# Two key buffers in the long-range attention, larger row and raw-weight rings in the last stage, first MLP chunk block by block

## The chip, the cores and the metric

The kernel runs on one core of one Trainium2 chip. The metric is the device time of one execution in microseconds (us); lower is better. A core has five engines that matter here: PE (TensorE, the matrix multiplier), DVE (VectorE), ACT (ScalarE), POOL (GpSimd) and SP (SyncE). Each runs its own list of instructions in order and waits on semaphores for the others. In this kernel SP issues every DMA, so it is one in-order queue for all loads and stores.

## The reference

One layer of a streaming encoder over a prompt of 2048 rows and a sample of 32 rows, width 1024, in float32:

```
z = rmsnorm(x) @ w_in                  # 3072 columns: q, k, v of group A and of group B
oa = diff_attn(qa, ka, va)             # 4 heads, two maps of 64 dims, values 128 wide, T5 bias,
                                       # weights = softmax(map 1) - lam * softmax(map 2), causal in chunks of 64
ob = band_attn(qb, kb, vb)             # 8 heads of 64, each chunk sees itself and 8 chunks before
h = x + concat(rmsnorm(oa)*(1-lam_init), rmsnorm(ob)) @ w_out
h = h + square(relu(rmsnorm(h) @ w_up)) @ w_down          # 1024 -> 4096 -> 1024
y = rmsnorm(h + sigmoid(h @ w_ple_gate) * (p @ w_ple_proj))
```

The sample attends to 128 cached keys and its own 32; y and the new keys and values are outputs.

## The kernel before

**Precision.** Every large matrix product is done with both operands split into a high part and a low remainder, and three matmuls per 128-deep slice (`mm3`, L186: hi·hi, hi·lo, lo·hi). A weight is therefore loaded raw (`wunit`, L177: tile "wr", two buffers), copied by ACT into the high part "wh" and subtracted by POOL, in pieces of 256 columns, into the low part "wl" (three buffers each). Activations are split in the same way: "cH"/"cL" for the MLP's input, "hH"/"hL" for the gate, "uh"/"ul" for the MLP's inner rows.

**Blocks.** The 2080 rows are four blocks (512, 512, 512, 544), taken as two halves, blocks 0 and 1, then 2 and 3. PE's product of one column block of 128 with one row block is 24 matmuls.

**Order.** The program text gives priorities; a scheduler with a timeline model writes the order of each engine's instructions once, when the program is built. On the chip each engine follows that order. So a change of a buffer count can move instructions of every engine, and SP's queue with them.

**Stages, in order of time.** Input norm and projections; short attention passes; band attention; then the long-range differential attention (`attn_a`, L511, with JA1 = [(4, 5), (6, 7, 8)] in pool a1), woven with the output projection, MLP and gate of the first half (about 1240 to 2080 us); then the last stage, from L1226: output projection of blocks 2 and 3 (`outproj`, L841), the gate of block 0 (`gate`, L988), the norms of blocks 2 and 3 (`cnorm`, L870), the MLP of both in 16 chunks (`mlp_up`, L917, `mlp_down`, L941), gate and final norm (`final`, L1039).

**Long-range attention.** `attn_a` runs each list of JA1 over the four heads g. A number j is a pair of query tiles of 128 rows (8 is the sample). For each head it loads the bias (ba), the keys (ka, hi and lo part on the two halves of the partitions; one buffer of 2 x 2208 columns; two or three DMAs per part) and then runs the pairs: queries (q, two buffers, four DMAs a pair), scores "s" (L567), maximum on DVE, exp on ACT, the difference of the two maps on DVE (L604), transposes, values (v), output "o". With (6, 7, 8) all 2208 keys are loaded, the last 160 (cache and sample) serving the sample alone. Eight passes, so seven changes from one head to the next.

**Rows of the last stage.** Tiles of one 128 x 544 row block, "tmp", form one ring of four. It is shared by the attention outputs that are to be split (`raw_o`, L802), the residual rows and squares of the output projection ("hd", L849, added on DVE at L860), the rows that the norm reads back (L879) and the MLP's relu results (L935).

**First MLP chunk.** `mlp_up` takes two columns f of 128 and both blocks of the half; the order is f, then block. So PE's order in the last stage is f0 of block 2, f0 of block 3, f1 of block 2, f1 of block 3. In the first half `mlp` is called with one block at a time.

Of the kernel before, what the change touches and what calls it, by code (L numbers as in the profile page):

```python
# [12 lines left out]
F32 = mybir.dt.float32  # L13
F32R = mybir.dt.float32r
# [5 lines left out]
P = 128  # L20
D = 1024
SP = 2048
SS = 32
# [110 lines left out]
class Kern:  # L134
    def __init__(self, tc, a):
        self.tc = tc
        self.nc = tc.nc
        self.a = a

    def dma(self, dst, src):  # L140
        if dst.dtype == F32R:
# [34 lines left out]

    def wunit(self, src, shape, hi_eng="act", lo_eng="pool"):  # L177
        nc = self.nc
        raw = self.wp.tile([P] + shape, F32, tag="wr", bufs=2, name="wr")
        self.dma(raw, src)  # L180
        hi = self.wp.tile([P] + shape, F32R, tag="wh", bufs=3, name="wh")
        lo = self.wp.tile([P] + shape, F32R, tag="wl", bufs=3, name="wl")
        self.split(hi, lo, raw, hi_eng, lo_eng)
        return hi, lo
# [326 lines left out]
    def attn_a(self, js, pool, ps_s, ps_t, ps_o):  # L511
        nc = self.nc
        last = 8 in js
        nk = KC if last else 256 * (js[-1] + 1)
        for g in range(4):
            ba = self.bias_a(pool, g)
            kt = pool.tile([P, 2, 1024 if self.small else KC], F32R, tag="ka", bufs=1, name="ka")
            for hl in range(2):
                src = self.kS[g, hl].rearrange("(m r) c -> r m c", m=2)
                for c0 in range(0, nk, 1024):  # L520
                    c1 = min(c0 + 1024, nk)
                    self.dma(kt[64 * hl : 64 * hl + 64, :, c0:c1], src[:, :, c0:c1])
            for j in js:
                self.attn_a_pair(g, j if j < 8 else None, kt, ba, pool, ps_s, ps_t, ps_o)

    def attn_a_pair(self, g, j, kt, ba, pool, ps_s, ps_t, ps_o):
        nc = self.nc
# [9 lines left out]
        for qi, t in enumerate(tiles):  # L537
# [25 lines left out]
            for bi, (k0, n, near) in enumerate(blocks):  # L563
                for m in range(2):
                    s = ps_s.tile([P, 512], F32, tag="s", name="s")[:nr, :n]
                    for hl in range(2):
                        nc.tensor.matmul(  # L567
                            s, q[:, m, hl, P * qi : P * qi + nr], kt[:, m, k0 : k0 + n], start=hl == 0, stop=hl == 1
                        )
                    dst = e[m][:nr, k0 - kb : k0 - kb + n]  # L570
                    nmx = nm[:nr, m, bi : bi + 1]
                    if near is None:
                        nc.vector.tensor_reduce(nmx, s, axis=AX.X, op=ALU.max, negate=True)  # L573
                        src = s
                    else:
                        nc.vector.tensor_tensor_reduce(
                            dst, s, ba[:nr, near : near + n], 1.0, -3e38, ALU.add, ALU.max, nmx
                        )
                        nc.vector.tensor_scalar(nmx, nmx, -1.0, None, op0=ALU.mult)
                        src = dst  # L580
                    nc.scalar.activation(dst, src, AF.Exp, bias=nmx, accum_out=z[:nr, m, bi : bi + 1])  # L581
# [218 lines left out]
                self.dma(self.pS[:, 1, k, t0 : t0 + n], lo[:, :n])  # L800

    def raw_o(self, wk, k, t0, n):  # L802
        t = wk.tile([P, BLK], F32, tag="tmp", bufs=4, name="oraw")[:, :n]
        self.dma(t, self.oT[:, k, t0 : t0 + n])
        return t

# [34 lines left out]
    def outproj(self, b, wk, oact, ps, acc):  # L841
        nc, a = self.nc, self.a
        n, t0 = BN[b], 512 * b
        W = a["w_out"][0]
        sq = wk.tile([P, BLK], F32, tag="acc", bufs=2, name="sqacc2")[:, :n]
        acc.append(sq)
        for d in range(8):
            wh, wl = self.wunit(W[:, P * d : P * d + P].rearrange("(k p) c -> p k c", p=P), [8, P])
            h = wk.tile([P, BLK], F32, tag="tmp", bufs=4, name="hd")[:, :n]  # L849
            self.dma(h, self.xT[:, d, t0 : t0 + n])  # L850
            for s0, sn in SUBS[b]:
                p = ps.tile([P, 512], F32, tag="mm", name="ops")[:, :sn]
                self.mm3(
                    p,
                    [
                        (wh[:, k], wl[:, k], oact[0][k][:, s0 : s0 + sn], oact[1][k][:, s0 : s0 + sn])
                        for k in range(8)
                    ],
                )
                nc.vector.tensor_tensor(h[:, s0 : s0 + sn], h[:, s0 : s0 + sn], p, op=ALU.add)  # L860
            if d == 0:
                nc.scalar.activation(sq, h, AF.Square)
            else:
                tmp = wk.tile([P, BLK], F32, tag="tmp", bufs=4, name="tmp")[:, :n]
                nc.scalar.activation(tmp, h, AF.Square)
                self.pool_tt(sq, sq, tmp, ALU.add)
            self.dma(self.hS[:, d, t0 : t0 + n], h)
            yield

    def cnorm(self, b, wk, act, out):  # L870
# [5 lines left out]
        r = wk.tile([P, BLK], F32, tag="r", bufs=2, name="rl")[:, :n]  # L876
        self.dma(r, self.rS[:, t0 : t0 + n])
        for k in range(8):
            tmp = wk.tile([P, BLK], F32, tag="tmp", bufs=4, name="tmp")[:, :n]  # L879
            self.dma(tmp, self.hS[:, k, t0 : t0 + n])  # L880
            nc.vector.scalar_tensor_tensor(
                tmp, tmp, self.g_mlp[:, k : k + 1], r, op0=ALU.mult, op1=ALU.mult
# [34 lines left out]
    def mlp_up(self, ch, nf, blocks, st, wk, up, mm):  # L917
        nc = self.nc
        Wu = self.a["w_up"][0]
        us = {}  # L920
        for f in range(nf):
            ft = nf * ch + f
            wh, wl = self.wunit(Wu[:, P * ft : P * ft + P].rearrange("(k p) c -> p k c", p=P), [8, P])
            for b in blocks:
                h, cH, cL = st[b]
                uh = up.tile([P, up.aw], F32R, tag="u", name="uh")
                ul = up.tile([P, up.aw], F32R, tag="u", name="ul")
                us[f, b] = (uh, ul)
                for s0, sn in SUBS[b]:
                    ps = mm.tile([P, 512], F32, tag="mm", name="ups")[:, :sn]  # L930
                    self.mm3(
                        ps,
                        [(wh[:, k], wl[:, k], cH[:, k, s0 : s0 + sn], cL[:, k, s0 : s0 + sn]) for k in range(8)],
                    )
                    r = wk.tile([P, BLK], F32, tag="tmp", bufs=4, name="relu")[:, :sn]  # L935
                    nc.scalar.activation(r, ps, AF.Relu)  # L936
                    nc.scalar.activation(r, r, AF.Square)
                    self.split(uh[:, s0 : s0 + sn], ul[:, s0 : s0 + sn], r, "act", "pool")
        return us

    def mlp_down(self, ch, nf, blocks, us, st, wk, mm):  # L941
# [154 lines left out]
    def run(self):  # L1096
        tc, nc, a = self.tc, self.nc, self.a
        with ExitStack() as top:
# [8 lines left out]
            cp = opened(top, "cp", 1)  # L1107
            self.dp = opened(top, "dp", 1, bass.MemoryType.DRAM)
            self.wp = opened(top, "wp", 3)
            mm = opened(top, "mm", MM, PSUM)  # L1110
            tp = mm
            psx = ExitStack()
# [112 lines left out]
            psx.close()  # L1225
            wk = opened(top, "wk4", 1)  # L1226
            fk = opened(top, "fk4", 1)
            self.gfin(fk)
            md = opened(top, "md", 8 - MM, PSUM, "right")
            act = Sized(opened(top, "acth", 4), BLK, True)  # L1230
# [75 lines left out]
```

## Time and profile before

| what | us |
| --- | --- |
| median of 3 runs | 3257.93 (3256.7 to 3264.15) |
| the profiled execution | 3256.49 |
| its span, first to last instruction | 3254.6 |
| PE busy in it | 3076.7 |
| DVE, ACT, POOL busy | 1557.3, 1693.7, 1706.8 |
| mean granted PE clock, as a share of full | 0.984 |

The time of a run is taken from outside; the span is what the profiler saw of one execution. A view of waits lists, for an engine, what its instructions waited for (tile, line, then the engine that let them go and what it wrote): total us, number of times, longest. A view of groups lists instructions of one line: count, busy time and mean ns, then idle time of the engine just before them with the releaser. A timeline gives start, length and instruction, with idle time before it in brackets. In a view of stretches each row is a piece of the span with the busy time of each engine, the granted PE clock (1.00 is full), the share of the DMA engines that was busy, and GB/s.

### The profile page before, as it was taken

The numbers are of one execution on the slowest core, as the hardware profiler recorded it, in microseconds if no ns is written. First come the engines' busy times: TensorE is split into PE (matmuls) and PEld (weight loads), VectorE is DVE, ScalarE is ACT, GpSimd is POOL, SyncE is SP. The second block draws the span as 40 slices with busy tenths as digits, with TensorE's granted clock in tenths as the row PEclk, the third lists the DMA queues.
The fourth block names the chain that finished last, engine by engine and source line by source line (L and its number), as shares of the span: only waits on it lengthen the run. The fifth ranks groups of instructions, "written<-read, shape, count | busy, mean of one in ns | idle before, by whom it ended". The sixth has DMA issues, their size and how long they took to land. (4 is left out here: it accounts for less than half of the span.)

```text
span 3254.6 us, 51557 instructions
## 1 busy us (share of the span) xinstructions
PE 3076.7 (95%) x17881; PEld 2692.7 (83%) x17881; DVE 1557.3 (48%) x3952; ACT 1693.7 (52%) x3717; POOL 1706.8 (52%) x2515
## 2 busy tenths in 40 slices
PE   6998999899999999999999999989899999999998
PEld 6877789789987887878788788868789999999988
DVE  5116786544465554676664565625442232223235
ACT  4226666776666765676665566544443222322245
POOL 5446766233245544565655455676854333433387
PEclk9999999999999999999999999999999999999999
DMA  7488786786788654554644544347531111111133
GB/s 232 165 259 246 226 244 206 213 259 202 215 239 229 187 146 118 152 156 138 199 122 135 137 123 136 121 143 233 150 113 46 46 46 46 46 46 46 47 94 103
DMA packets 519085, 489.02 MB, mean 150 GB/s; under 512 B 37885, under 2 KB 414017, under 8 KB 518825
## 3 DMA queue, kind: packets, MB, share of 16 engines
q1 hardware_dynamic: 518824, 485.73, 50.9%
q8 instruction: 142, 2.33, 0.3%
q14 instruction: 119, 0.97, 0.1%
HBM read 379.06 MB, written 110.49 MB: 150 GB/s over the span
## 5 line engine op out<-in xcount | busy, mean ns | idle before, releaser
L164 POOL TENSOR_TENSOR wl<-wr,wh 128x256 fp32r<-128x256 f32 x936 | 695.2, 774 | 489.4 <-ACT wh L169 453.1
L169 ACT ACTIVATE wh<-wr 128x1024 fp32r<-128x1024 f32 x338 | 357.2, 1057 | 598.5 <-PE dps L191 298.9
L971 DVE TENSOR_TENSOR h<-h,dps 128x512 f32<-128x512 f32 (+1 forms) x640 | 373.0, 585 | 575.0 <-PE dps L192 562.7
L154 POOL TENSOR_TENSOR wl<-wr,wh 128x256 fp32r<-128x256 f32 x416 | 301.8, 757 | 401.2 <-ACT wh L169 386.9
L190 PE MATMUL dps<-uh,wh 128*128 128x512 f32 (+1 forms) x1280 | 458.2, 358 | 7.1 <-DVE h L971 5.8
L190 PE MATMUL ups<-cH,wh 128*128 128x512 f32 (+1 forms) x1280 | 452.7, 354 | 5.7 <-ACT relu L936 4.5
L191 PE MATMUL ups<-cL,wh 128*128 128x512 f32 (+1 forms) x1280 | 451.5, 353 | 1.5 <-POOL cL L154 1.2
L192 PE MATMUL ups<-cH,wl 128*128 128x512 f32 (+1 forms) x1280 | 450.8, 352 | 0.0
L192 PE MATMUL dps<-uh,wl 128*128 128x512 f32 (+1 forms) x1280 | 450.1, 352 | 0.0
L191 PE MATMUL dps<-ul,wh 128*128 128x512 f32 (+1 forms) x1280 | 449.3, 351 | 0.0
L154 POOL TENSOR_TENSOR ul<-relu,uh 128x136 fp32r<-128x136 f32 (+1 forms) x320 | 198.9, 643 | 171.0 <-ACT uh L169 166.7
L190 PEld LDWEIGHTS dps<-uh,wh 128*128 128x128 f32 x1280 | 241.6, 189 | 39.7 <-DVE h L971 10.2
L190 PEld LDWEIGHTS ups<-cH,wh 128*128 128x128 f32 x1280 | 241.1, 188 | 38.6 <-ACT relu L936 4.7
L191 PEld LDWEIGHTS ups<-cL,wh 128*128 128x128 f32 x1280 | 241.6, 189 | 33.0 <-POOL cL L154 2.0
L192 PEld LDWEIGHTS dps<-uh,wl 128*128 128x128 f32 x1280 | 240.9, 188 | 33.6
L192 PEld LDWEIGHTS ups<-cH,wl 128*128 128x128 f32 x1280 | 241.3, 189 | 30.0
L191 PEld LDWEIGHTS dps<-ul,wh 128*128 128x128 f32 x1280 | 241.9, 189 | 26.5
L190 PE MATMUL qps<-aH,wh 128*128 128x512 f32 (+1 forms) x640 | 229.7, 359 | 11.0 <-ACT kr L432 3.4
L192 PE MATMUL qps<-aH,wl 128*128 128x512 f32 (+1 forms) x640 | 228.0, 356 | 0.0
L191 PE MATMUL qps<-aL,wh 128*128 128x512 f32 (+1 forms) x640 | 227.9, 356 | 0.0
L567 PE MATMUL s<-ka,q 128*128 128x256 f32 (+4 forms) x784 | 191.7, 346 | 30.8 <-DMA ka<-kS 10.1
L581 ACT ACTIVATE e<-s,nm 128x512 f32<-128x512 f32 (+3 forms) x256 | 154.9, 611 | 80.3 <-DVE nm L573 69.4
(218 smaller groups left out, 7075.0 us busy)
## 6 DMA issues: line engine op xcount, KB each, us to landing
wr<-w_up SPq DMA_DIRECT2D x96, 512.0 KB, 4.2
wr<-w_down SPq DMA_DIRECT2D x96, 512.0 KB, 3.8
wr<-w_in SPq DMA_DIRECT2D x74, 512.0 KB, 5.1
q<-qS SPq DMA_DIRECT2D x256, 128.0 KB, 4.3
v<-vSa SPq DMA_DIRECT2D x64, 512.0 KB, 3.9
ka<-kS SPq DMA_DIRECT2D x32, 512.0 KB, 7.7
wr<-w_out SPq DMA_DIRECT2D x32, 512.0 KB, 4.7
wr<-w_ple_gate SPq DMA_DIRECT2D x32, 512.0 KB, 4.4
```

Of the source, the lines that this page charges most:

```text
L154: nc.gpsimd.tensor_tensor(out[:, sl], a[:, sl], b[:, sl], op=op)
L164: nc.gpsimd.tensor_tensor(out[:, sl], a[:, sl], b[:, sl], op=op)
L169: nc.scalar.activation(hi, raw, AF.Copy)
L190: nc.tensor.matmul(ps, lh, rh, start=start and i == 0, stop=False)
L191: nc.tensor.matmul(ps, lh, rl, start=False, stop=False)
L192: nc.tensor.matmul(ps, ll, rh, start=False, stop=stop and i == n - 1)
L567: nc.tensor.matmul(s, q[:, m, hl, P * qi : P * qi + nr], kt[:, m, k0 : k0 + n], start=hl == 0, stop=hl == 1)
L581: nc.scalar.activation(dst, src, AF.Exp, bias=nmx, accum_out=z[:nr, m, bi : bi + 1])
L971: nc.vector.tensor_tensor(hv, hv, ps, op=ALU.add)
```

## The change

1. Keys in the long-range passes: the tile ka holds 2 x 2048 columns and has two buffers. The 160 cache and sample keys go into a tile of their own, ks, with one buffer, by as many DMAs as before. The early, short passes keep one buffer.
2. The ring "tmp" has eight tiles in the last stage (`self.nt`, 4 until then).
3. Raw weight tiles come from `self.rawp`; in the last stage it takes by turns from two rings of two tiles, one of them in the pool wk4. "wh" and "wl" keep three.
4. `mlp_up` for the first chunk takes all its columns for one block, then all for the next, and keeps both weights meanwhile. Later chunks keep the order column, then block.

The number of matmuls and of elementwise operations is unchanged.

```diff
--- before.py
+++ after.py
@@ -136,6 +136,7 @@
         self.tc = tc
         self.nc = tc.nc
         self.a = a
+        self.nt = 4
 
     def dma(self, dst, src):
         if dst.dtype == F32R:
@@ -176,7 +177,7 @@
 
     def wunit(self, src, shape, hi_eng="act", lo_eng="pool"):
         nc = self.nc
-        raw = self.wp.tile([P] + shape, F32, tag="wr", bufs=2, name="wr")
+        raw = self.rawp.tile([P] + shape, F32, bufs=2, name="wr")
         self.dma(raw, src)
         hi = self.wp.tile([P] + shape, F32R, tag="wh", bufs=3, name="wh")
         lo = self.wp.tile([P] + shape, F32R, tag="wl", bufs=3, name="wl")
@@ -511,17 +512,21 @@
     def attn_a(self, js, pool, ps_s, ps_t, ps_o):
         nc = self.nc
         last = 8 in js
-        nk = KC if last else 256 * (js[-1] + 1)
+        nk = SP if last else 256 * (js[-1] + 1)
         for g in range(4):
             ba = self.bias_a(pool, g)
-            kt = pool.tile([P, 2, 1024 if self.small else KC], F32R, tag="ka", bufs=1, name="ka")
+            kt = pool.tile([P, 2, 1024 if self.small else SP], F32R, tag="ka", bufs=1 if self.small else 2, name="ka")
+            if last:
+                ks = pool.tile([P, 2, PAST + SS], F32R, tag="ks", bufs=1, name="ks")
             for hl in range(2):
                 src = self.kS[g, hl].rearrange("(m r) c -> r m c", m=2)
                 for c0 in range(0, nk, 1024):
                     c1 = min(c0 + 1024, nk)
                     self.dma(kt[64 * hl : 64 * hl + 64, :, c0:c1], src[:, :, c0:c1])
+                if last:
+                    self.dma(ks[64 * hl : 64 * hl + 64], src[:, :, SP:KC])
             for j in js:
-                self.attn_a_pair(g, j if j < 8 else None, kt, ba, pool, ps_s, ps_t, ps_o)
+                self.attn_a_pair(g, j if j < 8 else None, kt if j < 8 else ks, ba, pool, ps_s, ps_t, ps_o)
 
     def attn_a_pair(self, g, j, kt, ba, pool, ps_s, ps_t, ps_o):
         nc = self.nc
@@ -565,7 +570,7 @@
                     s = ps_s.tile([P, 512], F32, tag="s", name="s")[:nr, :n]
                     for hl in range(2):
                         nc.tensor.matmul(
-                            s, q[:, m, hl, P * qi : P * qi + nr], kt[:, m, k0 : k0 + n], start=hl == 0, stop=hl == 1
+                            s, q[:, m, hl, P * qi : P * qi + nr], kt[:, m, k0 - kb : k0 - kb + n], start=hl == 0, stop=hl == 1
                         )
                     dst = e[m][:nr, k0 - kb : k0 - kb + n]
                     nmx = nm[:nr, m, bi : bi + 1]
@@ -800,7 +805,7 @@
                 self.dma(self.pS[:, 1, k, t0 : t0 + n], lo[:, :n])
 
     def raw_o(self, wk, k, t0, n):
-        t = wk.tile([P, BLK], F32, tag="tmp", bufs=4, name="oraw")[:, :n]
+        t = wk.tile([P, BLK], F32, tag="tmp", bufs=self.nt, name="oraw")[:, :n]
         self.dma(t, self.oT[:, k, t0 : t0 + n])
         return t
 
@@ -846,7 +851,7 @@
         acc.append(sq)
         for d in range(8):
             wh, wl = self.wunit(W[:, P * d : P * d + P].rearrange("(k p) c -> p k c", p=P), [8, P])
-            h = wk.tile([P, BLK], F32, tag="tmp", bufs=4, name="hd")[:, :n]
+            h = wk.tile([P, BLK], F32, tag="tmp", bufs=self.nt, name="hd")[:, :n]
             self.dma(h, self.xT[:, d, t0 : t0 + n])
             for s0, sn in SUBS[b]:
                 p = ps.tile([P, 512], F32, tag="mm", name="ops")[:, :sn]
@@ -861,7 +866,7 @@
             if d == 0:
                 nc.scalar.activation(sq, h, AF.Square)
             else:
-                tmp = wk.tile([P, BLK], F32, tag="tmp", bufs=4, name="tmp")[:, :n]
+                tmp = wk.tile([P, BLK], F32, tag="tmp", bufs=self.nt, name="tmp")[:, :n]
                 nc.scalar.activation(tmp, h, AF.Square)
                 self.pool_tt(sq, sq, tmp, ALU.add)
             self.dma(self.hS[:, d, t0 : t0 + n], h)
@@ -876,7 +881,7 @@
         r = wk.tile([P, BLK], F32, tag="r", bufs=2, name="rl")[:, :n]
         self.dma(r, self.rS[:, t0 : t0 + n])
         for k in range(8):
-            tmp = wk.tile([P, BLK], F32, tag="tmp", bufs=4, name="tmp")[:, :n]
+            tmp = wk.tile([P, BLK], F32, tag="tmp", bufs=self.nt, name="tmp")[:, :n]
             self.dma(tmp, self.hS[:, k, t0 : t0 + n])
             nc.vector.scalar_tensor_tensor(
                 tmp, tmp, self.g_mlp[:, k : k + 1], r, op0=ALU.mult, op1=ALU.mult
@@ -917,25 +922,29 @@
     def mlp_up(self, ch, nf, blocks, st, wk, up, mm):
         nc = self.nc
         Wu = self.a["w_up"][0]
-        us = {}
-        for f in range(nf):
+        us, w = {}, {}
+        order = [(f, b) for f in range(nf) for b in blocks]
+        if ch == 0:
+            order = [(f, b) for b in blocks for f in range(nf)]
+        for f, b in order:
             ft = nf * ch + f
-            wh, wl = self.wunit(Wu[:, P * ft : P * ft + P].rearrange("(k p) c -> p k c", p=P), [8, P])
-            for b in blocks:
-                h, cH, cL = st[b]
-                uh = up.tile([P, up.aw], F32R, tag="u", name="uh")
-                ul = up.tile([P, up.aw], F32R, tag="u", name="ul")
-                us[f, b] = (uh, ul)
-                for s0, sn in SUBS[b]:
-                    ps = mm.tile([P, 512], F32, tag="mm", name="ups")[:, :sn]
-                    self.mm3(
-                        ps,
-                        [(wh[:, k], wl[:, k], cH[:, k, s0 : s0 + sn], cL[:, k, s0 : s0 + sn]) for k in range(8)],
-                    )
-                    r = wk.tile([P, BLK], F32, tag="tmp", bufs=4, name="relu")[:, :sn]
-                    nc.scalar.activation(r, ps, AF.Relu)
-                    nc.scalar.activation(r, r, AF.Square)
-                    self.split(uh[:, s0 : s0 + sn], ul[:, s0 : s0 + sn], r, "act", "pool")
+            if f not in w:
+                w[f] = self.wunit(Wu[:, P * ft : P * ft + P].rearrange("(k p) c -> p k c", p=P), [8, P])
+            wh, wl = w[f]
+            h, cH, cL = st[b]
+            uh = up.tile([P, up.aw], F32R, tag="u", name="uh")
+            ul = up.tile([P, up.aw], F32R, tag="u", name="ul")
+            us[f, b] = (uh, ul)
+            for s0, sn in SUBS[b]:
+                ps = mm.tile([P, 512], F32, tag="mm", name="ups")[:, :sn]
+                self.mm3(
+                    ps,
+                    [(wh[:, k], wl[:, k], cH[:, k, s0 : s0 + sn], cL[:, k, s0 : s0 + sn]) for k in range(8)],
+                )
+                r = wk.tile([P, BLK], F32, tag="tmp", bufs=self.nt, name="relu")[:, :sn]
+                nc.scalar.activation(r, ps, AF.Relu)
+                nc.scalar.activation(r, r, AF.Square)
+                self.split(uh[:, s0 : s0 + sn], ul[:, s0 : s0 + sn], r, "act", "pool")
         return us
 
     def mlp_down(self, ch, nf, blocks, us, st, wk, mm):
@@ -1107,6 +1116,7 @@
             cp = opened(top, "cp", 1)
             self.dp = opened(top, "dp", 1, bass.MemoryType.DRAM)
             self.wp = opened(top, "wp", 3)
+            self.rawp = Rings((self.wp, "wr"))
             mm = opened(top, "mm", MM, PSUM)
             tp = mm
             psx = ExitStack()
@@ -1225,6 +1235,8 @@
             psx.close()
             wk = opened(top, "wk4", 1)
             fk = opened(top, "fk4", 1)
+            self.nt = 8
+            self.rawp = Rings((self.wp, "wr"), (wk, "wr"))
             self.gfin(fk)
             md = opened(top, "md", 8 - MM, PSUM, "right")
             act = Sized(opened(top, "acth", 4), BLK, True)
```

## The prediction

> **What bounds the kernel now.** I read the page first, then the busy time of each engine in stretches of 100 us, then the list of PE's waits in the two stretches that the change touches, then the timelines of PE, POOL and SP (the queue that issues every DMA, in order) around the longest of those waits.
>
> ```profile
> span 3254.6 us, 51557 instructions
> PE 3076.7 (95%) x17881; PEld 2692.7 (83%) x17881; DVE 1557.3 (48%) x3952; ACT 1693.7 (52%) x3717; POOL 1706.8 (52%) x2515
> ```
>
> PE is the bound: 3076.7 of 3254.6 us. The change adds and removes no matmul, so all it can win is PE's idle time and the half-speed clock that follows some of it. In the stretches (columns: length, then busy us and count of PE, PE's weight loads, DVE, ACT, POOL; then granted clock, DMA share, GB/s) the idle time sits in few places:
>
> ```profile
> 1500.00:1600.00 100.00, 93.75 (x454) 78.56 (x453) 70.39 (x144) 59.25 (x133) 59.75 (x77) 0.95 0.54 152
> ...
> 1800.00:1900.00 100.00, 91.81 (x457) 76.56 (x456) 61.31 (x132) 58.90 (x137) 53.23 (x78) 0.97 0.47 125
> ...
> 2200.00:2300.00 100.00, 90.90 (x564) 81.97 (x563) 42.37 (x70) 39.90 (x68) 71.44 (x97) 0.98 0.69 220
> 2300.00:2400.00 100.00, 83.70 (x406) 69.91 (x405) 48.74 (x61) 50.85 (x93) 86.17 (x112) 0.93 0.39 116
> ...
> 2500.00:3200.00 700.00, 700.00 (x4293) 632.18 (x4292) 203.76 (x388) 218.49 (x383) 314.75 (x489) 1.00 0.18 54
> ```
>
> The main MLP loop, 2500 to 3200, is full at full clock: nothing is to be had there, and in the built program PE's and POOL's orders in that loop do not change. Two stretches remain. **Long-range attention** (1240 to 2080), woven with the first half's MLP; PE's waits there:
>
> ```profile
> PE s L567 <- issue: 9.6, 2, 6.8
> PE s L567 <- DMA ka<-kS: 8.7, 4, 3.6
> ...
> PE s L567 <- DVE e L604: 3.1, 1, 3.1
> ```
>
> 9.6 + 8.7 + 3.1 = 21.4 us in seven waits. Their places in PE's timeline are the seven changes from one head to the next; five of them (start, length, instruction, in brackets the idle time before and who ended it):
>
> ```profile
> 1350.71 1.62 PE L567 MATMUL s<-ka,q 128*128 128x512 f32 x3 [3.12 <-DVE e L604]
> ...
> 1429.47 1.65 PE L567 MATMUL s<-ka,q 128*128 128x512 f32 x3 [3.65 <-DMA ka<-kS]
> ...
> 1506.73 0.50 PE L567 MATMUL s<-ka,q 128*128 128x512 f32 x1 [2.03 <-DMA ka<-kS]
> ...
> 1713.90 0.47 PE L567 MATMUL s<-ka,q 128*128 128x512 f32 x1 [2.86 <-issue]
> ...
> 1838.73 1.19 PE L567 MATMUL s<-ka,q 128*128 128x512 f32 x2 [6.75 <-issue]
> ```
>
> All are the first score matmul of a new head. "issue" and "DVE e" name engines that had long been done; what comes last is the keys and the queries, as SP's timeline before the longest one shows:
>
> ```profile
> 1822.64 3.87 SPq L145 DMA_DIRECT2D ka<-kS  x6
> 1826.55 7.97 SPq L145 DMA_DIRECT2D q<-qS  x6
> 1837.70 0.89 SPq L145 DMA_DIRECT2D wr<-w_down  x2
> ```
>
> The single key buffer comes free with the old head's last score; then six key loads and six query loads issue one after another, until 1834.52, and PE goes on at 1838.73. Weight loads for the MLP stand behind them.
>
> **Last stage up to the main loop** (2080 to 2420), PE's waits:
>
> ```profile
> PE gps L190 <- ACT wh L169: 11.8, 2, 10.5
> PE gps L190 <- DVE sm L1016: 7.7, 5, 4.6
> PE ops L190 <- DVE hd L860: 6.5, 3, 4.1
> PE ups L190 <- ACT relu L936: 4.5, 1, 4.5
> ...
> PE ops L190 <- ACT oact L169: 0.7, 1, 0.7
> PE ups L191 <- POOL cL L154: 0.7, 1, 0.7
> ...
> PE ops L192 <- POOL wl L164: 0.5, 1, 0.5
> ```
>
> The 7.7 belongs to the gate of block 1, which has two PSUM buffers and isn't touched.
>
> **The change, part by part.** *(1) Two key buffers, sample keys apart.* Removed: the wait of a head's key loads for the old head's last score. Added: nothing in count (the two 160-key pieces become loads of their own tile, ks). In the built program the key loads of head g+1 now stand about one head earlier in SP's queue, so they land tens of us before use. What is late next is the queries: their two buffers are unchanged. In the passes over (4,5) the queries of the new head's first pair can be loaded during the old head's second; nothing is left of the wait. In the passes over (6,7,8) that buffer is the one of pair 7, free only at its last score: four loads at some 7.97 / 6 = 1.33 us or less each, and a few us to land, while PE has the sample and the old head's value matmuls to do. PE's order puts the new score closer behind than before, so I leave 1.2 us at each of the three changes (between 0 and the mean of the seven, 3.06): 3.6 us. Gain 21.4 − 3.6 = 17.8 us.
>
> The added wait is that of ks (one buffer) for the old head's sample scores. Behind it in SP's queue stand query and value loads and MLP weights; before, the same loads stood behind six key loads that waited for the same score. I cost it at nothing, because that wait is no later than the one it replaces; if the cover is gone, it costs what the rival on weights below says.
>
> The clock also drops behind some of these waits:
>
> ```profile
> 1350.00:1354.00 4.00, 3.29 (x11) 2.84 (x12) 2.11 (x4) 0.00 (x0) 2.19 (x3) 0.57 1.11 234
> ...
> 1507.00:1511.00 4.00, 4.00 (x16) 3.56 (x16) 2.55 (x4) 1.04 (x2) 0.00 (x0) 0.57 1.10 278
> ...
> 1712.00:1718.00 6.00, 4.10 (x18) 3.40 (x19) 0.32 (x1) 0.60 (x1) 0.00 (x0) 1.00 1.08 206
> ```
>
> At 0.57 over 4 us a dip costs 4 × 0.43 = 1.7 us. With dips behind four of the seven (3.12, 3.65, 2.03 and 6.75 us) that would be 6.8 us more. I do not bank them: PE without its pauses meets its other inputs (weights, exponentials) sooner, which the trace of before cannot price, and which I bound by 0 and the same 6.8. So the two cancel. The Trainium skill, "TensorE: Matmul & The Clock Gate", section "Part 1: The HAM clock gate (the "warmup" mystery)", says that the clock halves after at least one idle window of about 3.4 us. This trace differs: a wait of 2.03 us was followed by a dip, one of 2.86 us by none. By the page only the 3.65 and the 6.75 would cost clock, 3.4 us in place of 6.8.
>
> *(2) and (3) Eight row tiles and four raw weight tiles in the last stage.* They act in two places. **Output projection** (ops rows): 6.5 + 0.7 + 0.5 = 7.7 us. DVE's add of the residual waits for its row:
>
> ```profile
> L860 DVE TENSOR_TENSOR hd<-hd,ops 128x272 f32<-128x272 f32 (+1 forms) x24 | 11.7, 517 | 39.1 <-DMA hd<-xT 35.1 <-PE ops L192 4.0
> ```
>
> 35.1 of DVE's 39.1 idle us there end with the load hd<-xT, which stands in SP's queue behind rows that wait for the ring of four, and behind weights that wait for two raw tiles. With eight and four these waits go; the oact tiles still alias memory that the final norm of block 1 holds until about then, so I leave 1 us. Gain 6.7.
>
> **Gate of block 0**, with the norm of blocks 2 and 3 beside it. PE's wait of 10.5 us is for the weights of the fifth gate column:
>
> ```profile
> 2315.88 3.73 SPq L145 DMA_DIRECT2D tmp<-hS  x4
> ...
> 2324.04 0.38 SPq L145 DMA_DIRECT2D wr<-w_ple_gate  x1
> ```
>
> They issue at 2324.04 because rows wait for the ring ahead of them. But POOL is nearly as late. Its chain began and PE's wait really ended here:
>
> ```profile
> 2300.33 2.83 POOL L164 TENSOR_TENSOR wl<-wr,wh 128x256 fp32r<-128x256 f32 x4 [3.40 <-ACT wh L169]
> ...
> 2334.61 0.39 PE L192 MATMUL gps<-hH,wl 128*128 128x512 f32 x1
> ```
>
> The first matmul with the fifth column's wl runs at 2334.61. The clock is low until there:
>
> ```profile
> 2326.00:2334.60 8.60, 6.09 (x16) 4.87 (x17) 7.24 (x8) 4.57 (x7) 8.60 (x10) 0.56 0.61 183
> ```
>
> PE's 6.09 busy us at 0.56 hold 6.09 × 0.44 = 2.7 us that full clock would save, so the loss is 10.5 + 2.7 = 13.2 us. Between 2300.33 and 2334.61 POOL does 16 pieces of wl, 6 of sig, 4 of h and 8 of cL:
>
> ```profile
> L164 POOL TENSOR_TENSOR wl<-wr,wh 128x256 fp32r<-128x256 f32 x144 | 113.2, 818 | 27.9 <-ACT wh L169 22.5 <-PE ops L192 5.4
> L154 POOL TENSOR_TENSOR sig<-sm,sig 128x256 f32<-128x256 f32 x32 | 26.7, 855 | 1.4 <-DVE sm L1016 1.4
> L154 POOL TENSOR_TENSOR h<-h,sig 128x256 f32<-128x256 f32 x32 | 25.2, 808 | 11.2 <-DVE sig L1034 11.2
> ...
> L154 POOL TENSOR_TENSOR cL<-tmp,cH 128x256 fp32r<-128x256 f32 (+2 forms) x20 | 15.4, 799 | 0.0
> ```
>
> 16 × 0.818 + 6 × 0.855 + 4 × 0.808 + 8 × 0.799 = 27.8 us of the 34.3, and none of it goes. What goes is POOL's waiting: the 3.40 us at the head of the chain, and part of what 34.3 − 27.8 leaves inside it, 6.5 us. In the built program the first two gate weights also stand one output column sooner in SP's queue, so that up to one set of wl pieces (2.83 us) can be done before the chain's old start. 3.40 + 2.83 + about a third of 6.5 is 8.4; I take 8 of the 13.2 as won, 5.2 stay. Bounds: 0 (POOL fills up with cL pieces, as the rows come sooner) and 13.2.
>
> *(4) First MLP chunk block by block.* PE's first MLP chunk waits 4.5 + 0.7 = 5.2 us because columns of block 3 are asked for while its norm is still being split. Block 2 first gives the norm of block 3 about two column passes. But POOL has its cL as well as the weights, so I leave 1.5. Gain 3.7; bounds 0 and 5.2. The same number of matmuls; the two weights are held longer, in three slots as before.
>
> Part (4) and the ring sizes leave the main loop alone; at the tail (after 3200) the order shifts a little, which I bound by ±1 us and cost at nothing.
>
> **Sum.** 17.8 + 6.7 + 8 + 3.7 = 36.2 us, 18.4 of it in the last stage. The profiled execution took 3256.5 us, its span and 1.9 around it: 3220.3. The median of the runs shown is 1.4 us above it; I state **3220**.
>
> **Rivals.**
> *A. POOL holds the last stage.* The gate of block 0 and the first chunk lose what they did; only attention and output projection gain, 24.5 us: 3232. For: POOL is busy 86.17 of 100 us from 2300. Against: its 3.40 us wait at the head of the chain is for a load.
> *B. Weights late in the attention stage.* PE's pauses move from the scores to the MLP matmuls; gain only in the last stage, 18.4: 3238. For: weights stand behind keys and queries in one queue (1837.70 behind 1822.64, 15 us). Against: the keys ahead of them no longer wait.
> *C. Slower, by the same queue.* If ks or a query, waiting for a late score, holds the weights long enough that PE loses more per head change than it does now, the stage turns from gain to loss. Now the mean is 21.4 / 7 = 3.06 us. To eat the last stage's 18.4 it must be 3.06 + 18.4 / 7 = 5.7 us, and to be 0.3% (9.8 us) slower 3.06 + 28.2 / 7 = 7.1 us at each of seven changes: 3266. The longest single wait now is 6.75, so this needs every change to be worse than today's worst.
> *D. The change doesn't do what it says.* The queries, not the keys, come last everywhere, and the gate's chain is POOL's: both stages stay, 3254 to 3258. For: at 1838.73 the queries were issued after the keys. Against: four of the seven waits are named as the keys'.
> *E. Everything goes.* 21.4 + 6.8 clock + 7.7 + 13.2 + 5.2 = 54.3 us, and a dip of 1.7 each at the output projection and the first chunk (an estimate from the dips above): 57.7 us, 3199.
>
> **How the numbers follow.** Forecast 0.50, A 0.12, B 0.09, E 0.11, D 0.10, C 0.08. The bound of what can be told from no change is 0.3%, 9.8 us. Faster by more: 0.50 + 0.12 + 0.09 + 0.11 = 0.82; within: 0.10 (D); slower: 0.08 (C). The range leaves out C and D: from E, less 4 us for the tail's 1 and the spread of the runs, 3195, to B without the gate's 8 and with the tail's 1, 3247.
>
> **What would show it.** Part 1: PE's waits in L567 for ka or "issue" gone from 1240 to 2080, and no dip of the clock behind those places; left over, short waits for q at the three changes of (6,7,8). If dps or ups wait for wh or wl there instead, it is B or C. Output projection: no DVE L860 wait for hd<-xT. Gate of block 0: the fifth column's wait about 5 us, POOL without idle time ahead of it; if it is still over 10, A. First chunk: wait for relu under 2 us. The prediction is wrong if the attention stage does not end at least 10 us sooner against the start of it, or if the main loop is no longer full.

## The result and the profile after

| kernel | median us | runs | ratio to before | 95% interval |
| --- | --- | --- | --- | --- |
| before | 3257.31 | 3256.5 to 3264.15 (4) | | |
| changed | 3238.57 | 3235.06 to 3241.03 (4) | 0.9935 | 0.992 to 0.995 |

The change gains 18.7 us by the medians (0.58%; by the ratio in the table 0.65%). The forecast was 3220, a gain of 36: the direction and the range hold, the size is half. The page of the changed kernel's profile:

```profile
span 3235.4 us, 51443 instructions
PE 3075.5 (95%) x17881; PEld 2690.7 (83%) x17881; DVE 1568.3 (48%) x3952; ACT 1693.0 (52%) x3717; POOL 1715.2 (53%) x2515
```

PE has the same work; 18 of the 19 us that the span lost were PE's idle time. The same stretches of 100 us as before:

```profile
1500.00:1600.00 100.00, 94.08 (x478) 78.61 (x477) 76.84 (x165) 65.27 (x153) 63.12 (x83) 1.00 0.58 163
...
1800.00:1900.00 100.00, 98.32 (x513) 82.89 (x512) 63.27 (x136) 63.15 (x149) 53.16 (x78) 1.00 0.50 137
...
2200.00:2300.00 100.00, 95.62 (x582) 85.31 (x581) 47.66 (x64) 47.91 (x79) 85.25 (x108) 1.00 0.75 233
2300.00:2400.00 100.00, 84.56 (x440) 71.48 (x440) 57.68 (x80) 45.96 (x94) 70.33 (x99) 0.93 0.37 119
```

The two stretches of the attention stage are fuller and at full clock; 2300 to 2400 is as empty as it was (84.56 against 83.70). PE's waits in the attention stage, 1240 to 2080 (total, times, longest):

```profile
PE dps L191 <- DVE h L980: 9.3, 10, 1.7
PE dps L191 <- ACT wh L170: 5.1, 1, 5.1
PE s L572 <- DMA q<-qS: 2.5, 3, 1.2
```

No wait for ka, no "issue" of more than 0.2. In the last stage, 2080 to 2420:

```profile
PE pps L191 <- DVE sm L1025: 8.5, 2, 5.7
PE ups L191 <- ACT relu L945: 8.1, 1, 8.1
PE gps L191 <- DVE sm L1025: 7.7, 5, 4.7
PE ops L191 <- ACT oact L170: 3.3, 2, 2.1
PE ops L191 <- ACT wh L170: 1.7, 1, 1.7
```

The 11.8 us for the gate's weights and the 6.5 for hd are gone. In their place stand a wait of 5.7 us for sm in the gate of block 0 (the 8.5 holds 2.8 that block 1's gate had before), and the wait in the first MLP chunk, which grew from 4.5 to 8.1. Both end with DVE: the relu that PE waits for, which is written into a tile of the ring "tmp" as the norm's rows are, stood 6.27 us on ACT for DVE's cL. ACT, DVE and POOL at that place, three timelines of the changed kernel:

```profile
2351.27 0.60 ACT L945 ACTIVATE relu<-ups 128x512 f32<-128x512 f32 x1 [6.27 <-DVE cL L176]
```

```profile
2338.33 13.48 DVE L176 TENSOR_TENSOR cL<-tmp,cH 128x544 fp32r<-128x544 f32 x2 [5.21 <-ACT cH L170]
2351.74 0.68 DVE L1025 TENSOR_SCALAR sm<-gps 128x512 f32<-128x512 f32 x1
2352.34 1.34 DVE L176 TENSOR_TENSOR cL<-tmp,cH 128x544 fp32r<-128x544 f32 x2
```

```profile
2337.27 1.44 POOL L155 TENSOR_TENSOR sig<-sm,sig 128x256 f32<-128x256 f32 x2
2338.66 6.48 POOL L155 TENSOR_TENSOR cL<-tmp,cH 128x181 fp32r<-128x181 f32 x12
2345.10 5.49 POOL L165 TENSOR_TENSOR wl<-wr,wh 128x256 fp32r<-128x256 f32 x8
```

Two cL on DVE take 13.48 us where the next two take 1.34. They begin under POOL's sig, and POOL then runs 20 instructions without a pause, at its full pace (6.48 / 12 = 0.54 us), until 2350.59. The view of this line's instructions in that stretch (minimum, median, maximum in ns) says that it is one of them:

```profile
L176 DVE TENSOR_TENSOR cL<-tmp,cH x4: 707/710/12852, 2338.3 to 2353.0; 128x544 fp32r<-128x544 f32 x4
```

That one ends at 2351.18, 0.58 us after POOL's last instruction; alone such a cL takes 0.71 us. So it stood until POOL stopped. In the kernel before, the same four took 1.1 to 1.26 us each beside POOL, in turn with it.

**By stages.** Executions differ by several us before the change begins: a fixed matmul of the first half's MLP (the 81st of the form ups<-cH,wh) starts at 1212.79 in the kernel before and at 1218.43 in the changed one, though PE's order up to there is the same; over all profiles of this study it starts between 1210.4 and 1223.1. So the tables below give stages: *attention*, from that matmul to the first of block 1's gate (2109.66 before, 2096.60 after), and *last*, from there to the first of block 2's gate (3115.68, 3096.71).

| | attention | last |
| --- | --- | --- |
| before | 896.9 | 1006.0 |
| changed | 878.2 | 1000.1 |
| gain | 18.7 | 5.9 |
| forecast | 17.8 | 18.4 |

### The profile page after: what moved, and what is told of

Its sections match the earlier page's. It is cut to its first block, busy times and chain, and to the rows that moved or that the text cites. A ratio compares the mean times of both kernels' runs of the same rounds, so it can differ in the third digit from the quotient of the medians.

```text
span 3235.4 us, 51443 instructions
## 1 busy us (share of the span) xinstructions
PE 3075.5 (95%) x17881; PEld 2690.7 (83%) x17881; DVE 1568.3 (48%) x3952; ACT 1693.0 (52%) x3717; POOL 1715.2 (53%) x2515
## 4 chain that ended last, share of the span: by engine, by line
PE 54%; DVE 5%; DMA 4%; ACT 2%; issue 1%; POOL 1%; SPq 0%; DVEq 0%; POOLq 0%; ACTq 0%
PE ups L191 7%; PE dps L191 7%; PE ups L192 7%; PE ups L193 7%; PE dps L192 7%; PE dps L193 7%; PE s L572 2%; PE gps L191 1%; PE gps L192 1%; PE gps L193 1%; DMA wr<-w_down 1%; PE tpp L644 1%; DVE e L609 1%; PE ob L771 1%; PE o L659 1%
## 5 line engine op out<-in xcount | busy, mean ns | idle before, releaser
L572 PE MATMUL s<-ka,q 128*128 128x512 f32 (+3 forms) x768 | 184.0, 341 | 11.1 <-DMA q<-qS 3.7
```

The costliest lines, as they stand in the source:

```text
L572: nc.tensor.matmul(s, q[:, m, hl, P * qi : P * qi + nr], kt[:, m, k0 - kb : k0 - kb + n], start=hl == 0, stop=hl == 1)
```

## Experiments: each part alone, and each left out

Theory after the result: the key buffers gave what was forecast; in the last stage the loads came sooner as forecast, but DVE became late. Rivals: the parts are worth what I forecast and something else cost the time; or one part of the last stage costs what another gains.

**Keys only.** `self.nt = 8` made 4, the second raw ring and the chunk order taken back.

> The changed kernel with the last stage as before (four row tiles, two raw weight tiles, first MLP chunk column by column): only the two key buffers. Theory (the attention stage gave most of the gain, the last stage little): between the gate of block 1 and 1212 us the profile of the changed kernel gained 18.7 us, so 3257 - 19 = 3238, or 3257 - 13 = 3244 if the 5.6 us that its first 700 us lost belong to the change and not to the execution. No PE wait for ka; the wait of dps for wh of 5.1 us at the first head change is there again. Rival (my prediction's sizes: 17.8 and 18.4): 3239 here too, but then the last stage alone must also give 18.

Measured: 3245.39 us, ratio 0.9957 (0.9943 to 0.9971), a gain of 13.5. Attention 884.0, last 1006.0, as before. The waits of before in the gate and in the first chunk are there again (the wait for hd is 1.9 and not 6.5, beside 2.4 for oact and 2.1 for wl):

```profile
PE gps L191 <- ACT wh L170: 11.2, 2, 10.4
...
PE ups L191 <- ACT relu L945: 4.5, 1, 4.5
```

**Last stage only.**

```
-            kt = pool.tile([P, 2, 1024 if self.small else SP], F32R, tag="ka", bufs=1 if self.small else 2, name="ka")
-            if last:
-                ks = pool.tile([P, 2, PAST + SS], F32R, tag="ks", bufs=1, name="ks")
+            kt = pool.tile([P, 2, 1024 if self.small else KC], F32R, tag="ka", bufs=1, name="ka")
...
-                if last:
-                    self.dma(ks[64 * hl : 64 * hl + 64], src[:, :, SP:KC])
```

> The changed kernel with one key buffer as before: only eight row tiles, four raw weight tiles and the first chunk block by block. Theory: the last stage gives 6 us (14.9 - 12.5 in the output projection, 6.2 in the gate of block 0, -2.5 in the first chunk), so 3251; PE's waits pps for sm (5.7) and ups for relu (8.1) are there. Rival (my prediction): 18.4 us, 3239.

Measured: 3250.98 us, ratio 0.9979 (0.9967 to 0.9991), a gain of 7.9. Attention 893.2, last 1000.0. It has both new waits (5.6 for sm, 8.6 for relu), so the key buffers have no part in them. 13.5 and 7.9 add up to 21.4, the change's 18.7 within the runs' spread: nothing here shows that one part needs the other, and the rival's 18 for the last stage falls.

**Four row tiles, all else as changed** (`self.nt = 4`).

> The changed kernel with four row tiles in the last stage, all else kept. Theory (eight row tiles let the norm's row work onto DVE early, ahead of the gate's sm, and beside unbroken POOL work): the waits pps for sm 5.7 and ups for relu 8.1 go or shrink below 5 together, and the output projection's wait for hd comes back (7): about even, 3234 to 3242. Rival (the larger row ring is what gains in the last stage, the rest does nothing): 6 to 10 us slower than the changed kernel, 3245 to 3249.

Measured: 3235.48 us, ratio 0.9929 (0.9914 to 0.9944). Attention 881.6, last 999.0. The wait for sm falls from 5.7 to nothing, but 4.6 for the gate's weights are back, at the same output column, the fifth; and the wait in the first chunk is still 7.3. The wait for hd, which I expected back at 7, is 0.9. So the time came out as expected and the waits only in part: the ring of eight does not make the wait for relu, and whether it makes the one for sm can't be told where PE stands for weights at the same place.

**The old chunk order, all else as changed.**

```
-        if ch == 0:
+        if False:
             order = [(f, b) for b in blocks for f in range(nf)]
```

> The changed kernel with the first MLP chunk column by column as before, all else kept. Theory (the 8.1 us wait of ups for relu is DVE's cL held up beside POOL's unbroken run, whatever the order of the chunk): the wait stays within 2 us or grows, same time or up to 3 us slower. Rival (the new order makes the wait, since it asks for two tiles of one block before the rows are done): the wait falls to the 4.5 us of before, 3 to 4 us faster.

Measured: 3238.03 us, ratio 0.9934 (0.991 to 0.9957); last 998.7, against 1000.1 with the new order, so with both rings larger the new order gains nothing. The wait stays, and here the profile names its end directly:

```profile
PE ups L192 <- DVE cL L176: 7.4, 1, 7.4
```

**Two raw tiles, all else as changed.**

> The changed kernel with two raw weight tiles in the last stage, all else kept. Theory (the four raw tiles are what the last stage gained from; the ring of eight and the chunk order add nothing): from the start of block 1's gate to that of block 2's the stage takes 1004 to 1007 us against 1000.1 with four (1006.0 in the kernel before), and PE's wait gps for wh of about 10 us in the gate of block 0 is back. Rival (the row ring alone takes the gate's loads out of the queue): the wait stays under 5 us and the stage within 2 us of 1000.

Measured: 3235.35 us, ratio 0.9925 (0.991 to 0.994); last 996.6. The theory of this run, that the four raw tiles made the gain, is wrong: the wait for the gate's weights is 4.3, not 10, and the stage is 3.5 us shorter than with four. Its rival was right on the wait, and 1.4 us beyond its 2 us on the stage. The wait for relu is 8.3.

**Keys and four raw tiles alone.** `self.nt = 4` and the old order.

> Two key buffers and four raw weight tiles alone; four row tiles and the old order of the first chunk. Theory (these two are all that gains): the last stage as the changed kernel or up to 3 us better, 997 to 1000.1 us, total 3232 to 3238. Rival (the parts need each other): 4 us or more slower than the changed kernel, above 3242.

Measured: 3245.89 us, ratio 0.9953 (0.9938 to 0.9968); attention 879.7, last 1007.6. Wrong as well: with the four raw tiles alone the last stage is 1.6 us longer than before. It waits 4.7 for weights, and then in the first chunk 3.8 + 3.8 + 3.0 for cL, relu and cH. Against the run with four row tiles this kernel differs in the chunk order alone, and its last stage is 8.6 us longer (1007.6 against 999.0): with four row tiles the new order is worth that, with eight nothing. The parts of the last stage don't add up. Either larger ring alone takes the wait for the gate's weights from about 11 to 4.3 to 4.7 us, both take it to nothing; but either alone already brings the held cL on DVE (9.31 to 13.09 us in these runs).

## Experiments: what holds DVE

**All low parts of the last stage's norm rows on DVE.**

```
-            self.split(cH[:, k, :n], cL[:, k, :n], tmp, "act", "dve" if k % 2 else "pool")
+            self.split(cH[:, k, :n], cL[:, k, :n], tmp, "act", "dve" if k % 2 or self.nt == 8 else "pool")
```

> The changed kernel with all low parts of the last stage's norm rows on DVE, none on POOL. Theory (a DVE instruction with two SBUF inputs stands as long as POOL runs on without a pause: 12.85 us for one cL behind 12 cL and 8 wl pieces on POOL): POOL's runs end sooner, since its next sig waits for DVE's sm; the longest cL on DVE falls from 12.85 to under 9, and PE's wait in the first chunk from 8.1 to under 5; but eight more cL of 0.7 to 1.2 us stand ahead of sm, so the gate's wait for sm (5.7) stays or grows: 0 to 4 us faster than the changed kernel. Rival (DVE is late because it has too much work): eight more cL make both waits longer, 5 us or more slower.

Measured: 3228.05 us (3227.4 to 3228.39), ratio 0.9903 (0.9886 to 0.9919); last 987.0, 13.1 us shorter than in the changed kernel. DVE has twice as many cL in that place and is done sooner, since none is held:

```profile
L176 DVE TENSOR_TENSOR cL<-tmp,cH x8: 709/1257/1267, 2337.8 to 2345.7; 128x544 fp32r<-128x544 f32 x8
```

POOL's instructions beside them take 1.22 us each in place of 0.73: the two engines go in turn. What is left of the new waits is 0.9 for sm and 2.4 for POOL's wl; the wait for relu is gone. The rival (DVE has too much work) falls: more work on DVE, and 13 us less. The theory had the direction; its 0 to 4 us were far too small, since it counted on a shorter hold and there is none.

**The first chunk's weight remainders on DVE** (`lo_eng="dve"` for the two w_up weights of the first chunk).

> The changed kernel with the low parts of the first MLP chunk's two w_up weights of the last stage on DVE in place of POOL. Theory (the lock lasts as long as POOL's run): POOL's run is 12 cL and 4 wl pieces in place of 12 and 8, 6.5 + 2.8 = 9.3 us, so the longest cL on DVE is about 10 and not 12.85; PE's wait in the first chunk 5 to 7. Rival (load of DVE): the two weights add 2 to 5 us on DVE, the wait grows beyond 8.1.

Measured: 3234.61 us, ratio 0.992 (0.9906 to 0.9935); last 992.8. Neither expectation: no cL is held at all.

```profile
L176 DVE TENSOR_TENSOR cL<-tmp,cH x4: 991/1020/1078, 2344.0 to 2347.7; 128x544 fp32r<-128x544 f32 x4
```

```profile
2345.53 8.94 POOL L155 TENSOR_TENSOR cL<-tmp,cH 128x181 fp32r<-128x181 f32 x12
```

POOL has the same unbroken run of 12 cL, in 8.94 us and not 6.48, and DVE's cL go between. So a long run of POOL is not enough to hold DVE: the two go in turn in one program and not in the other. The wait for relu is 1.1, the one for sm 5.7, as in the changed kernel.

**All low parts on POOL** (the same line with "dve" taken away in the last stage).

> The changed kernel with all low parts of the last stage's norm rows on POOL, none on DVE. Theory (the 12.85 us of one cL on DVE was DVE standing while POOL ran on without a pause): there is no cL left to stand, but POOL's run grows by 8 x 0.54 to 0.73 us a block; the other DVE work with two SBUF inputs (the norm's products) may stand instead, up to 15 us. PE's wait in the first chunk ends on POOL's cL: 4 to 10 us, last stage 996 to 1004 us. Rival (that cL was slow by itself, by its shape or place): the wait goes, last stage 987 to 992.

Measured: 3243.84 us, ratio 0.9947 (0.9932 to 0.9961); last 1002.9. No cL on DVE, no DVE instruction of the last stage is held, and the wait for relu is down to 1.5 in two pieces; but POOL is now late, by 3.3 in the first chunk (cL and wl) and most of all in the gate:

```profile
PE gps L193 <- POOL wl L165: 9.1, 1, 9.1
```

The time is in the theory's range and the mechanism only half its: most of the wait moved from the first chunk to the gate's weights, which stand behind POOL's cL. This is the POOL chain of the forecast (rival A) in pure form.

**Low parts on DVE and two raw tiles; low parts on DVE and four row tiles; low parts on DVE and neither ring nor order.**

> All low parts of the last stage's norm rows on DVE, as in the run with the whole ring change, but two raw weight tiles. Theory (without the hold of DVE the rings add what their own loads allow; two raw tiles had a shorter output projection of block 2): last stage 983 to 990 us against 987.0 with four raw tiles, total 3224 to 3231. Rival (four raw tiles are needed for the gate of block 0): PE's wait gps for wh 4 us or more longer, last stage above 991.

> As the changed kernel with all low parts of the last stage's norm rows on DVE, but a ring of four row tiles (four raw weight tiles and the new chunk order kept). Theory (eight row tiles help once DVE is not held): 2 to 6 us slower than with eight, last stage 989 to 993. Rival (the larger row ring adds nothing): within 2 us of 987.0.

> Two key buffers and all low parts of the last stage's norm rows on DVE; four row tiles, two raw tiles and the old order of the first chunk. Theory (row loads stand in the queue ahead of the gate's weights with a ring of four, whoever does the low parts): PE's wait of 10 us in the gate of block 0 shrinks only by what POOL has less to do, 3 to 6 us; last stage 998 to 1003 against 1006.0 before. Rival (moving the low parts is the whole of it, the rings add nothing): 987 to 990.

| low parts on DVE, with | median us | ratio, interval | last |
| --- | --- | --- | --- |
| 8 rows, 4 raw, new order | 3228.05 | 0.9903, 0.9886 to 0.9919 | 987.0 |
| 8 rows, 2 raw, new order | 3230.47 | 0.9905, 0.9889 to 0.9922 | 986.2 |
| 4 rows, 4 raw, new order | 3226.94 | 0.9900, 0.9885 to 0.9915 | 987.2 |
| 4 rows, 2 raw, old order | 3238.96 | 0.9937, 0.9916 to 0.9957 | 1003.5 |

The last row has the old wait for the gate's weights again:

```profile
PE gps L191 <- ACT wh L170: 10.5, 2, 8.6
...
PE ups L192 <- DVE cL L176: 1.7, 2, 1.2
```

So the rings and the new order together are worth 16 us here (1003.5 to 987), moving the low parts alone 2.5 (1006.0 to 1003.5), and one larger ring does as well as two. The order's share of the 16 is not shown: no run with the low parts on DVE has a larger ring and the old order. The expectation that eight row tiles beat four fails. That two raw tiles do as well holds for the time, though the wait for weights that its rival named is there (5.9 us). In the last kernel the longest wait for weights shrank by 1.9 us and not by 3 to 6 (10.5 to 8.6), and the stage is just above the expected 998 to 1003. The first three kernels are faster than the kernel before, and their last stages are 13 to 14 us shorter than the changed kernel's; they can't be told from one another.

## Why the forecast was right in direction and too large

**Two key buffers: right.** All seven head-change waits are gone. Queries are late at three places, 2.5 us in all where I left 3.6. The clock dips behind those waits are gone too, in stretches around the same times:

```profile
1428.00:1433.00 5.00, 4.57 (x22) 3.53 (x21) 4.29 (x9) 4.14 (x14) 4.45 (x7) 1.00 0.72 200
1507.00:1511.00 4.00, 4.00 (x20) 3.31 (x19) 3.21 (x9) 1.86 (x8) 3.65 (x6) 1.00 0.34 95
```

I had let that 6.8 us cancel against PE meeting its other inputs sooner. It nearly did: over the stage PE's idle time fell by 12.9 us (35.6 to 22.7), and the time that the same 4378 matmuls took fell by 5.8 (861.2 to 855.4). The cancelling was a choice between two bounds, so 18.7 beside 17.8 is in part luck. The waits of dps for h are 9.3 and not 5.8, and 5.1 are new, for the weights of one MLP step, with a dip of the clock of their own (0.50 from 1294 to 1300). That is rival B once, in the first head, and SP's timeline shows it, first of the kernel before, then of the changed one:

```profile
1270.60 3.16 SPq L145 DMA_DIRECT2D q<-qS  x4
1273.87 1.05 SPq L145 DMA_DIRECT2D wr<-w_down  x2
```

```profile
1276.41 3.01 SPq L146 DMA_DIRECT2D q<-qS  x4
1279.46 4.54 SPq L146 DMA_DIRECT2D ka<-kS  x4
1284.04 1.26 SPq L146 DMA_DIRECT2D ks<-kS  x2
1285.41 1.04 SPq L146 DMA_DIRECT2D wr<-w_down  x2
```

The early loads of the second head's keys and of ks now stand ahead of the weights; from 1279.46 to 1285.41 are 6 of the 11.5 us by which they issue later. The rest is no cost of the change: this execution was 5.6 us later already at 1218.43, and the queries are 5.8 later. The first of the weights then took 10.1 us to land, and 7.3 before. All 12 kernels of the study with two key buffers have this wait, at 4.8 to 5.5 us; the two without don't. The stage's gain was 18.7 in this pair of profiles; over the 12 kernels the mean is 880.7 us (878.2 to 884.0), over the two with one buffer 895.1: 14.3. The runs of keys only say 13.5. So 17.8 was some 4 too much, about the size of the weights' wait, which I had cost at nothing.

**Output projection: 6.7 forecast.** The wait for hd went, as forecast. New ones came at once: 3.3 for oact, 1.7 for wh and 0.9 for wl where I had left 1. From the start of block 1's gate to the start of block 0's the time fell by 3.3 us (179.6 to 176.3).

**Gate of block 0: 8 forecast, with 5.2 left by POOL.** The wait for weights went altogether, so the POOL chain was not what stayed. What stayed, 5.7 us, is DVE, whose list has norm work ahead of the gate's sm; that it comes near the 5.2 is luck. DVE's timeline there, between two sm:

```profile
2302.62 0.68 DVE L1025 TENSOR_SCALAR sm<-gps 128x512 f32<-128x512 f32 x1
2303.22 0.42 DVE L915 TENSOR_TENSOR sqacc<-sqacc,r 128x272 f32<-128x272 f32 x1
2303.57 2.35 DVE L176 TENSOR_TENSOR cL<-tmp,cH 128x512 fp32r<-128x512 f32 x2
2305.84 1.56 DVE L916 TENSOR_SCALAR sqacc<-sqacc 128x272 f32<-128x272 f32 x2
2307.32 1.83 DVE L917 TENSOR_TENSOR r<-r,sqacc 128x272 f32<-128x272 f32 x2
2309.08 0.68 DVE L1025 TENSOR_SCALAR sm<-gps 128x512 f32<-128x512 f32 x1
```

DVE is never idle and the second sm stands behind 6.2 us of norm work (the four lengths added). These are the third and fourth sm of the gate, and norm work between them is not new. DVE's timeline of the kernel before has 7.6 us between the same two:

```profile
2321.42 0.68 DVE L1016 TENSOR_SCALAR sm<-gps 128x512 f32<-128x512 f32 x1
2322.02 3.00 DVE L881 SCALAR_TENSOR_TENSOR tmp<-tmp,g_mlp_s,rl 128x512 f32<-128x512 f32 x3
...
2326.76 2.34 DVE L175 TENSOR_TENSOR cL<-tmp,cH 128x512 fp32r<-128x512 f32 x2
2329.03 0.68 DVE L1016 TENSOR_SCALAR sm<-gps 128x512 f32<-128x512 f32 x1
```

There PE stood for the fifth column's weights from 2318.0 to 2328.5, and the fourth sm, done at 2329.71, came in time for it. In the runs with one larger ring PE stands 4.3 to 4.7 for weights at that column, and waits 0.5 at most for sm. The shorter wait for weights uncovered the one for DVE. From the start of the gate to a fixed matmul early in the chunk (the 521st ups<-cH,wh) the time fell by 5.0 us (75.3 to 70.3). I named the right stage and the wrong engine. My sum for POOL's chain was wrong too: POOL was busy 31.4 of the 34.3 us and not 27.8, because its instructions take longer there than the means that I used (four wl 3.54 to 3.77 us, and 2.83 at the head of the chain), so the 6.5 us of slack inside it were 2.9.

**First chunk: 3.7 forecast, 2.5 lost** (60.7 to 63.2 us from there to the 601st). This is the step that failed. I set the cover of block 2's columns against POOL's cL and never asked what POOL's unbroken run does to DVE. The wait is DVE's held cL. In the six kernels with a cL of 9 us or more on DVE, PE waits 7.3 to 8.6 us there, or 10.6 in three pieces (keys and four raw tiles); in the kernels with a ring enlarged and none held so long, at most 1.7 in one wait. Moving the low parts to DVE gave back 13.1 of the last stage, 9.5 of them here (63.2 to 53.7) and 2.7 in the gate; the stage then gains 19.0 against the kernel before.

**What was shown and what not.** That DVE stood as long as POOL ran is shown by the records: in six kernels one cL took 9.31 to 13.39 us beside 14 to 22 POOL instructions, and ended 0.58 us after the last of them each time. That the hold decides the first chunk is shown by the runs without it: PE's idle time in that stretch is 8.4 to 12.1 us in those six, 1.6 to 3.5 in the three with low parts on DVE and a larger ring and in the one with the weights' remainders on DVE. With all low parts on POOL it is 6.3, and POOL is late there. Why the pair goes in turn in some programs and holds in others is open: in the kernel before, in the run with the weights' remainders on DVE and in that with all low parts on DVE, the same DVE form met POOL's instructions and took turns. Each of the six held cL came after DVE had been idle for 4.6 us or more, but so did the first one of the kernel before (5.4 us), which took turns. The main loop and the tail are unchanged, as forecast (690.4 and 690.3 from the 601st ups to block 2's gate; 139.0 and 138.7 after it).

## What to carry to other kernels

A load that waits for its only buffer at each change of head is worth a second buffer, and its price is that the early loads stand ahead of something else in the same queue: look what that is. When you clear the wait that ends last, ask for every engine near it what it will do with the inputs that now come sooner, and in what order it has them in its list; here 5.7 us for DVE had stood unseen behind 10.5 for weights at the same place. Where two engines can hold each other up, think twice before giving them the two halves of one elementwise job: here all of it on DVE took 13 us off the last stage, all of it on POOL none.

## What the runs showed of the hardware

A DVE subtract of two SBUF rows of 544 takes 0.71 us alone, 1.0 to 1.27 us when POOL's elementwise instructions run beside it and the two go in turn (POOL's then take 1.04 to 1.24 us in place of 0.54 to 0.74), and up to 13.4 us when it is held until a run of POOL's ends. The Trainium skill, "SBUF — State Buffer", section "Who interferes with whom", says that a DVE instruction with two SBUF inputs contends with a GpSimd instruction that reads SBUF; the traces agree (1.0 to 1.27 us beside POOL, 0.71 alone), and show that the hold can last over 20 GpSimd instructions. It isn't tied to the last stage: in four profiles (keys only is one) a DVE e<-e,c of 384 columns at about 552 us took 3.67 to 3.70 us beside five POOL instructions, and in the ten others, of the same instruction order up to there, 0.75 to 0.76:

```profile
552.75 3.70 DVE L609 SCALAR_TENSOR_TENSOR e<-e,c 128x384 f32<-128x384 f32 x1 [0.87 <-ACT e L608]
```

In the four it began 0.09 to 0.11 us after a POOL instruction had begun, in the ten 0.39 to 0.40 us after. So whether DVE is let in also turns on where the two happen to meet in an execution. For the cL rows this offset doesn't part the two cases: the six held ones began 0.10 to 0.50 us into a POOL instruction, and others that began 0.11 to 0.45 us into one took turns.
